# A two-layer encoder trunk on one core: the first layer's last columns as a pair, the V chunk first in the second mixer, and more of the couples' sums made ahead

## The chip, the cores and the metric

The kernel runs on one core of one Trainium2 chip, as one program. The metric is the device time of one execution in microseconds, the lower the better. TensorE is PE in the profile (PEld is its weight load), VectorE is DVE, ScalarE is ACT, GpSimd is POOL, and SyncE, which issues nearly all DMAs here, is SP.

## The reference, cut to what matters

The trunk has two layers on a sequence of 256 tokens with 2048 features, all float32. Layer 0 mixes tokens with a bidirectional mLSTM (8 heads), layer 1 with a bidirectional HGRN2 (16 heads). Behind each mixer stands a gated MLP of 5504 features with a convolution of width 3.

```python
def conv_glu(hn, w_up, conv_w, conv_b, w_down):
    u = hn @ w_up
    a, v = jnp.split(u, 2, axis=-1)
    ...
    c = conv_b
    for j in range(CONV_W):
        c = c + ap[:, j:j + s] * conv_w[j]
    return (jax.nn.gelu(c, approximate=False) * v) @ w_down

def reference(...):
    ...
    for layer in range(DEPTH):
        hn = rmsnorm(h, norm_mix_g[layer])
        if layer % N_MIXERS == 0:
            mix = mlstm_mixer(hn, ...)
        else:
            mix = hgrn_mixer(hn, ...)
        h = h + mix
        h = h + conv_glu(rmsnorm(h, norm_ffn_g[layer]), ffn_w_up[layer], ...)
    return rmsnorm(h, final_g)
```

The HGRN2 mixer projects its input to q, i (the values V), g (an output gate), and one forget gate for each direction. A forget gate f gives `k = (1 - lb) * sigmoid(-f)` and the decay `lb + (1 - lb) * sigmoid(f)`.

## The kernel before

**Products in two parts.** Every matrix product is made with operands that are split in two float32r parts, a high one and a low one, and three matmuls: high by high, high by low, low by high. Weights come from HBM as float32 (`raw`, 1 MB at a time, three buffers), ScalarE casts a piece of 128 x 1024 to the high part (`wh`, L144), and VectorE subtracts that from the piece (`wl`, L145). `LOOK = 3` such pieces are prepared ahead of TensorE.

**Chunks.** `stream` runs through a list of chunks, in the order in which TensorE executes them; each has a kind:

- "fm" (feature-major): 256 output features by 256 tokens, the weights stationary; for each k tile and each half of the features one matmul of 512 columns (L340) and one of 256 (L344). The entries of `swap` exchange two neighbours in this order.
- "tm" (token-major): 256 tokens by 512 output features, x stationary, 6 matmuls of 512 columns for each k tile (L356).
- "st" (a pair): 256 tokens by 1024 output features. Two k tiles by two blocks of 512 columns by two halves of the tokens form a unit. A plain unit takes 8 products of three matmuls; a unit listed in `seven` takes 7, by the scheme of Strassen and Winograd with 2 x 2 blocks (L231). For that it needs sums of the weight's blocks (the couples' sums, T1 to T4) and sums of the token blocks of x (`token_sums`, `SX`). Four PSUM banks (`psm`) hold the products P1, P6, P7, P5 that several outputs share, the four banks of the other pool (`psa`) the outputs' own sums. Behind the last unit of seven `mid` adds the shared products to the residual `hm` (L557 to L565); at the end `done` adds the rest (L570).

**The couples' sums** are either made in the pair itself, by `combine` (four subtractions on VectorE, L203), or ahead: `prepare` is a side job that loads a unit's four blocks (2 x 0.5 MB, `praw`), subtracts on VectorE (L603) and stores the result to a scratch tensor in HBM, `tscr`; the pair loads it again (`T<-tscr`). Before the change 22 units of layer 0 and 30 of layer 1 are made ahead, in lists: `early[layer]` runs beside the mixer of that layer (`prepare_early`), and each of the two parts of a layer's MLP has a list that runs beside its up chunks. The three units of each mixer's own pair (`SEVEN_MIX`) are made by `combine`.

**Side jobs.** Everything that isn't a chunk's main product is a Python generator on `Side`, and `side.tick` gives each its turn as the chunks are written, by a clock of planned microseconds (10.4 for an fm chunk). The periods of `prepare` and the steps of a head are in that time. The framework then schedules each engine's instructions; only those that are pinned keep their written order.

**The order of the work.** Layer 0: 16 chunks of the mixer; its output projection as a tm chunk, a pair for the middle 1024 columns (`mixed`), and a tm chunk; then the MLP in two parts of 22 and 21 tiles of 128 features (`FA`, `FB`): up chunks (fm), then the down projection over the part's tiles. In the first part this is a pair for columns 0 and 1 (of four of 512) and a pair for columns 2 and 3. In the second part it is a pair for columns 0 and 1 with six units of seven, and **two tm chunks** for columns 2 and 3 (`w_d2`). Layer 1 begins with its mixer (`hgrn`): four groups of four heads, each with six fm chunks, a V chunk after the third of them, and a G chunk after the sixth. Its output projection and its MLP follow as in layer 0, except that the last part ends in a second pair (`w_d3`) with seven units of seven.

**Norms.** When a column block of `hm` is final, `Norm.add` squares it on ScalarE (L509) and starts `turn`, which transposes it on TensorE (L417) into a bank of `psa` and splits it into the next x tiles, `xt` (ScalarE L362, VectorE L363). While a pair is running (`held`), `turn` waits, since the pair has all of `psa`.

**A head of the second mixer** takes its three projections (`take`), makes the gate `g` with a Sigmoid on ScalarE (L978) and a multiply-add on VectorE (L980), multiplies q by it on GpSimd (L981), then doubles its window seven times on VectorE (L1029), and ends in small matmuls.

Of the kernel before, what the change touches and what calls it, by code (L numbers as in the profile page):

```python
# [8 lines left out]
F32 = mybir.dt.float32  # L9
# [6 lines left out]
P = 128  # L16
T = 256
# [32 lines left out]
SEVEN = (1, 2, 3, 4, 6, 7, 8, 9), (1, 2, 4, 5, 7, 8)  # L50
SEVEN_END = (1, 2, 3, 4, 5, 6, 7)
# [4 lines left out]
QUAD = 32  # L56
LEVELS = (1, 2, 4, 8, 16, 32, 64)
# [5 lines left out]
def trunk_kernel(ctx, tc, xT, x_d, fg_d, pp_d, cst_d, w_gate, w_first, w_aq, w_ak, w_av, w_ao, w_aout, w_ao2,  # L63
                 w_bq, w_bv, w_bg, w_bout, w_bo2, w_up, w_d0, w_d1, w_d2, w_d3, out, mscr, tscr):
# [21 lines left out]
    def aux(name):  # L86
        return psa.tile([P, 512], F32, tag="aux", name=name)
# [40 lines left out]
    turns = dict(w=0)  # L128
# [92 lines left out]
    def squares_by_seven(ch, fetch, ready):  # L221
# [37 lines left out]
        for u in range(units):  # L259
# [27 lines left out]
            if u in ch.seven:  # L287
# [8 lines left out]
                if u == last:  # L296
                    ch.mid(psm_)
                continue
# [82 lines left out]
    class Norm:  # L381
# [166 lines left out]
    def pair(src, nk, c0, x, sums, norm, seven):  # L548
# [18 lines left out]
        def done(ps):  # L567
            for i in range(4):
                h = part(i // 2, i % 2)
                dve.tensor_tensor(h, h, ps[i], ALU.add)  # L570
            if norm is not None:
                norm.add(c0)
                side.push(second())
# [7 lines left out]
        ch.stored, ch.waits, ch.pool = {}, None, None  # L581
        return ch

    def prepare(tiles, todo, first, period, finished, start, ahead):
# [12 lines left out]
        for i, (_, dst) in enumerate(todo):  # L597
# [21 lines left out]
    def mixed(w, w2, x, norm, close):  # L619
# [8 lines left out]
        two = pair(w2, KT, 1, x, sums, norm, SEVEN_MIX)  # L628

# [299 lines left out]
    def hgrn(norm, nxt):  # L929
# [32 lines left out]
        def take(hd, what, ps):  # L962
# [17 lines left out]
            dve.tensor_scalar(g, g, oml[:, hd:hd + 1], lb[:, hd:hd + 1], ALU.mult, ALU.add)  # L980
# [110 lines left out]
        swaps = {(0, 1): (0, 6), (1, 0): (2, 24), (1, 2): (4,), (2, 0): (2, 24), (2, 2): (4,), (3, 0): (2,), (3, 2): (10,)}  # L1091
        heads = [dict() for _ in range(BH)]
        chunks = []
        for qd in range(BH // 4):
# [25 lines left out]
            chunks.append(Chunk("tm", w_bg[qd], KT, norm.x, done_g, paced=True))  # L1120
# [5 lines left out]
        return chunks + mixed(w_bout, w_bo2, yx, nxt, stack.close)  # L1126


    def ffn(layer, norm, nxt):
        stack = ExitStack()  # L1130
        ending = isinstance(nxt, FinalNorm)
        seven = SEVEN[0], SEVEN_END if ending else SEVEN[1]
        box = dict(n=(2 * len(SEVEN[0]) + len(SEVEN[1])) * layer)
        chunks, pairs = [], []
# [9 lines left out]
        def done_up(f, i, GT, SX, seven):  # L1144
            def go(ps):
# [18 lines left out]
                if i % 2 and i // 2 in seven:  # L1164
                    n = seven.index(i // 2)
                    if seven is not SEVEN[1]:
                        z = GT[i - 1][:, P:T], GT[i - 1][:, T + P:2 * T]
                    else:
                        if n % 3 == 0:
                            box["s4"] = mp.tile([P, 768], F32R, tag=f"sx{len(seven) + n // 3}", name="s4")  # L1170
                        z = tuple(box["s4"][:, (n % 3 * 2 + j) * P:(n % 3 * 2 + j + 1) * P] for j in range(2))
# [4 lines left out]
        for part, (f0, nf) in enumerate(((0, FA), (FA, FB))):  # L1176
            GT, SX, todo, finished = [], {}, [], []

# [7 lines left out]
            for i in range(nf):  # L1186
                chunks.append(Chunk("fm", w_up[layer, f0 + i], KT, norm.x, done_up(f0 + i, i, GT, SX, seven[part]),
# [150 lines left out]
```

## Time and profile before

| | us |
|---|---|
| median of 3 runs (lowest, highest) | 2385.79 (2384.44, 2386.21) |
| the profiled execution | 2384.87 |
| its span, first to last instruction | 2382.9 |
| TensorE busy in the span | 2365.6 |
| VectorE busy | 1938.4 |
| ScalarE busy | 1433.6 |
| GpSimd busy | 205.4 |

Stretches of the span, in us from its start: mixer 0 to 392 (its pair 326 to 367), up chunks of layer 0's first part 392 to 638, their pairs to 746, up chunks of the second part to 980, its pair to 1032, the two tm chunks to 1092, mixer 1 to 1608, its pair to 1656, up chunks of layer 1's first part 1680 to 1926, pairs to 2035, up chunks of the second part to 2268, pairs to the end.

In a row of the windows, the figures are: the stretch, its length, the busy time of PE, PEld, DVE, ACT and POOL with the number of instructions in brackets, the granted TensorE clock as a share, the share of time in which the DMA engines were busy, and GB/s. With one engine or one line asked for, its busy time alone stands there. In a row of the groups: line, engine, operation, output and inputs by the program's names, shapes, number; busy us, mean ns; idle us before them and who ended it. In a row of the timeline: start, us, engine, line, and in square brackets the idle time before. A wait's row has the total, the number and the longest.

### The profile page before, as it was taken

How to read it: one execution, taken by the hardware profiler on the slowest of the kernel's cores; microseconds unless marked ns; L12 is line 12 of the kernel's file. 1: busy time of each engine (PE TensorE's matmuls, PEld its weight loads, DVE VectorE, ACT ScalarE, POOL GpSimd, SP SyncE). 2: the span in 40 equal slices, each digit the busy share in tenths (PEclk: the TensorE clock that was granted, in tenths of full speed). 3: DMA queues.
4: the chain of work that ended last, by engine and by line, in shares of the span. 5: the costliest groups of instructions: out<-in, count | busy, mean ns of one | idle time of the engine just before them, and what ended most of it. 6: DMA issues, size and time to landing. Idle time of an engine off the chain costs nothing.

```text
span 2382.9 us, 38182 instructions
## 1 busy us (share of the span) xinstructions
PE 2365.6 (99%) x14572; PEld 2024.3 (85%) x14572; DVE 1938.4 (81%) x3001; ACT 1433.6 (60%) x2271; POOL 205.4 (9%) x242
## 2 busy tenths in 40 slices
PE   9999999999999999999999999999999999999998
PEld 7888888888888888888888888887888888888886
DVE  7777687888788887766888888888788788888787
ACT  7655456555665555655666666665555566455565
POOL 0100000000000000001233222320000000000000
PEclk9999999999999999999999999999999999999999
DMA  8777656886697885755666666764788588887695
GB/s 300 240 272 268 227 174 214 302 303 226 223 354 272 283 280 195 274 190 204 244 234 228 246 236 227 245 225 173 258 299 283 195 309 310 288 288 253 204 345 201
DMA packets 112471, 601.23 MB, mean 252 GB/s; under 512 B 12688, under 2 KB 13200, under 8 KB 66464
## 3 DMA queue, kind: packets, MB, share of 16 engines
q1 hardware_dynamic: 110592, 594.78, 71.1%
q0 software_dynamic: 1120, 3.21, 0.8%
q8 instruction: 114, 1.87, 0.3%
q10 hardware_dynamic: 576, 0.79, 0.1%
q14 instruction: 69, 0.57, 0.1%
HBM read 542.05 MB, written 56.69 MB: 251 GB/s over the span
## 4 chain that ended last, share of the span: by engine, by line
PE 95%; DVE 2%; DMA 1%; issue 1%; ACT 0%; SPq 0%; POOL 0%; DVEq 0%; POOLq 0%; ACTq 0%
PE mm L340 36%; PE mm L356 18%; PE mm L344 18%; PE pc L231 12%; PE mm L231 6%; DMA praw<-in_w_d 1%; PE py L1066 1%; PE pn L808 1%; DVE wl L145 1%; PE pd L1016 0%; PE pz L417 0%; PE pa L1016 0%; DVE QK L1029 0%; DMA Mb<-mscr 0%; DMA raw<-in_w_first 0%
## 5 line engine op out<-in xcount | busy, mean ns | idle before, releaser
L340 PE MATMUL mm<-xt,wh 128*128 128x512 f32 x3776 | 1314.2, 394 | 0.0
L145 DVE TENSOR_TENSOR wl<-raw,wh 128x1024 fp32r<-128x1024 f32 (+1 forms) x845 | 1034.6, 1229 | 274.6 <-ACT wh L144 268.9
L144 ACT CAST wh<-raw 128x1024 fp32r<-128x1024 f32 (+1 forms) x845 | 875.6, 1042 | 520.4 <-PE mm L340 293.6
L344 PE MATMUL mm<-xt,wl 128*128 128x256 f32 x3776 | 1046.3, 278 | 0.0
L340 PEld LDWEIGHTS mm<-xt,wh 128*128 128x128 f32 x3776 | 706.2, 188 | 160.1
L344 PEld LDWEIGHTS mm<-xt,wl 128*128 128x128 f32 x3776 | 709.7, 188 | 4.5 <-issue 0.4
L356 PE MATMUL mm<-wh,xt 128*128 128x512 f32 x1024 | 320.5, 391 | 2.2 <-ACT xt L362 1.6
L231 PE MATMUL pc<-wh,g 128*128 128x512 f32 x676 | 228.0, 389 | 0.0
L356 PEld LDWEIGHTS mm<-wh,xt 128*128 128x128 f32 x1024 | 191.1, 188 | 41.8 <-ACT xt L362 2.0
L356 PE MATMUL mm<-wl,xt 128*128 128x512 f32 x512 | 197.9, 391 | 0.0
L603 DVE TENSOR_TENSOR praw<-praw 128x512 f32<-128x512 f32 x208 | 143.8, 691 | 49.4 <-DMA praw<-in_w_d 39.0
L231 PEld LDWEIGHTS pc<-wh,g 128*128 128x128 f32 x676 | 126.9, 188 | 26.4
L231 PE MATMUL pc<-wl,g 128*128 128x512 f32 x338 | 131.5, 389 | 0.0
L145 DVE TENSOR_TENSOR wl<-T,wh 128x1024 fp32r<-128x1024 f32 (+1 forms) x116 | 110.2, 961 | 20.2 <-ACT wh L144 19.5
L231 PE MATMUL mm<-wh,sx 128*128 128x512 f32 x348 | 124.4, 391 | 0.0
L144 ACT CAST wh<-T 128x1024 fp32r<-128x1024 f32 (+1 forms) x116 | 96.2, 836 | 45.8 <-PE pc L231 20.3
L564 POOL TENSOR_TENSOR hm<-hm,u 128x512 f32<-128x512 f32 x9 | 12.6, 1395 | 1186.4 <-DVE u L563 592.3
L1029 DVE TENSOR_TENSOR QK<-QK,G 128x256 f32<-128x256 f32 x224 | 109.7, 537 | 5.4 <-ACT kq L1008 5.0
L356 PEld LDWEIGHTS mm<-wl,xt 128*128 128x128 f32 x512 | 96.2, 188 | 19.1
L1150 ACT COPY avc<-mm 128x256 f32<-128x256 f32 x172 | 64.2, 373 | 78.2 <-PE mm L344 78.2
L1008 ACT COPY kq<-QK 128x512 f32<-128x512 f32 x112 | 74.5, 669 | 57.3 <-DVE QK L1029 44.6
L1151 DVE TENSOR_TENSOR avc<-mm,avc 128x256 f32<-128x256 f32 x172 | 71.9, 418 | 12.7 <-ACT avc L1150 12.6
(247 smaller groups left out, 2322.3 us busy)
## 6 DMA issues: line engine op xcount, KB each, us to landing
raw<-in_w_up SPq DMA_DIRECT2D x172, 1024.0 KB, 5.4
praw<-in_w_d SPq DMA_DIRECT2D x104, 512.0 KB, 6.8
tscr<-praw SPq DMA_DIRECT2D x104, 512.0 KB, 6.8
raw<-in_w_bq SPq DMA_DIRECT2D x48, 1024.0 KB, 5.0
raw<-in_w_d SPq DMA_DIRECT2D x52, 768.0 KB, 6.1
T<-tscr SPq DMA_DIRECT2D x52, 768.0 KB, 7.7
raw<-in_w_d SPq DMA_DIRECT2D x32, 1024.0 KB, 5.2
raw<-in_w_ao SPq DMA_DIRECT2D x24, 1024.0 KB, 4.9
```

What stands on the lines that cost most here:

```text
L144: pin(act.copy(wh[:, :m], r))
L145: pin(dve.tensor_tensor(wl[:, :m], r, wh[:, :m].bitcast(F32), ALU.subtract))
L231: pe.matmul(ps, a, b, start=id(ps) not in begun, stop=stop and i == 2)
L340: pe.matmul(ps[f], wh[:, c:c + P], x, start=k + kk == 0, stop=False)
L344: pe.matmul(ps[f][:, 0:T], wl[:, c:c + P], x[:, 0:T], start=False, stop=k + kk == ch.nk - 1)
L356: pe.matmul(ps[t], x[:, a + t * P:a + (t + 1) * P], w[:, c], start=st and i == 0, stop=sp and i == 2)
L603: dve.tensor_tensor(out, x, y, ALU.subtract)
L808: pe.matmul(pn[:, 0:258], w, v, start=(i == 0), stop=(i == len(parts) - 1))
L1008: act.copy(m, blocks(QK, h))
L1029: dve.tensor_tensor(two[:, j], two[:, j], by[:, j], ALU.mult)
L1150: act.copy(z, p[:, T:2 * T])
L1151: dve.tensor_tensor(z, p[:, 0:T], z, ALU.add)
```

## The change

1. Layer 0's last two tm chunks become a pair (`w_d3` for both layers; `w_d2` goes), with seven units of seven; the pair before it has seven instead of six. `SEVEN` is now the same for both layers.
2. `SPLIT` says in which lists the last pair's units are made ahead: in layer 0 none beside the mixer, 2 beside the first part's up chunks, 5 beside the second's; in layer 1 2, 2 and 3 (before: 7 beside the mixer). The three units of mixer 1's pair are now made ahead too, in `early[1]`. In numbers, layer 0's lists go from 8, 8, 6 to 8, 10, 12, layer 1's from 15, 8, 7 to 13, 10, 10.
3. `prepare` spreads a list over all of its time: the last third of a period, which only `prepare_early` waited for, is waited for everywhere.
4. Since layer 0's last pair gives two column blocks at once, `turn` may use the four banks of `psm` once the last unit of seven is behind it (`ch.rest`), and `done` calls `norm.add` for the first block as soon as that one is added.
5. In the second mixer the V chunk of the first group comes first, and V and G chunks stand ahead of the fm chunks with the numbers in `TMS`; `swap` is set by the same list. From the third V chunk on the order of the chunks is the one before.
6. The gate's multiply-add moves from VectorE to ScalarE.
7. In the mixers' pairs the temporaries of `combine` and of `token` get buffers of their own.

```diff
-SEVEN = (1, 2, 3, 4, 6, 7, 8, 9), (1, 2, 4, 5, 7, 8)
-SEVEN_END = (1, 2, 3, 4, 5, 6, 7)
+SEVEN = (1, 2, 3, 4, 6, 7, 8, 9), (1, 2, 3, 4, 5, 6, 7)
+SPLIT = (0, 2, 5), (2, 2, 3)
...
+TMS = (0, 4, 8, 11, 15, 18, 21)
...
     def temporary(pool_, name):
-        return pool_.tile([P, 1536], F32, tag="avc", bufs=TEMP if pool_.name == "ff" else 2, name=name)
+        ff = pool_.name == "ff"
+        return pool_.tile([P, 1536], F32, tag="avc" if ff else name, bufs=TEMP if ff else 2, name=name)
...
-        side.until(lambda: ch.waits is None or ch.waits)
+        side.until(lambda: all(ch.waits))
...
                 if u == last:
                     ch.mid(psm_)
+                    ch.rest = ch.ends
...
         def turn(self, c):
             yield 2.5
-            while held:
+            while held and not held[-1].rest:
                 yield 1.0
             for k0 in (4 * c, 4 * c + 2):
-                pz = aux("pz")
+                pz = psm.tile([P, 512], F32, tag="mm", name="pz") if held else aux("pz")
...
         def done(ps):
-            for i in range(4):
-                h = part(i // 2, i % 2)
-                dve.tensor_tensor(h, h, ps[i], ALU.add)
+            for c in range(2):
+                for t in range(2):
+                    h = part(t, c)
+                    dve.tensor_tensor(h, h, ps[2 * t + c], ALU.add)
+                if norm is not None and c == 0:
+                    norm.add(c0)
             if norm is not None:
-                norm.add(c0)
                 side.push(second())
...
             for j in range(2):
                 nc.sync.dma_start(dst[:, j * 1024:(j + 1) * 1024], loaded[i][j])
+            yield period / 3
             if not ahead:
-                yield period / 3
                 load(i + 1)
...
+    def store(ch, src, u, todo):
+        ch.stored[u] = tscr[turns["t"]]
+        turns["t"] += 1
+        todo.append((src[:, 2048 * u:2048 * (u + 1)], ch.stored[u]))
+
-    def mixed(w, w2, x, norm, close):
+    def mixed(w, w2, x, norm, close, layer=None):
...
         two = pair(w2, KT, 1, x, sums, norm, SEVEN_MIX)
+        if layer is not None:
+            for u in SEVEN_MIX:
+                store(two, w2, u, early[layer][0])
+            two.waits = [early[layer][1]]
...
-            dve.tensor_scalar(g, g, oml[:, hd:hd + 1], lb[:, hd:hd + 1], ALU.mult, ALU.add)
+            act.activation(g, g, AF.Identity, bias=lb[:, hd:hd + 1], scale=oml[:, hd:hd + 1])
...
-        swaps = {(0, 1): (0, 6), (1, 0): (2, 24), (1, 2): (4,), (2, 0): (2, 24), (2, 2): (4,), (3, 0): (2,), (3, 2): (10,)}
...
+            vs.append(Chunk("tm", w_bv[qd], KT, norm.x, done_v, begin if qd == 0 else None, paced=True))
+            gs.append(Chunk("tm", w_bg[qd], KT, norm.x, done_g, paced=True))
             for i in range(6):
-                if i == 3:
-                    chunks.append(Chunk("tm", w_bv[qd], KT, norm.x, done_v, paced=True))
...
-                chunks.append(Chunk("fm", w_bq[6 * qd + i], KT, norm.x, done_i, begin if not chunks else None,
-                                    swap=swaps.get((qd, i), (1, 13) if i == 3 else ()), paced=True))
+                n = 6 * qd + i
+                fs.append(Chunk("fm", w_bq[n], KT, norm.x, done_i, swap=(2, 13) if n in TMS else (4, 15), paced=True))
...
-            chunks.append(Chunk("tm", w_bg[qd], KT, norm.x, done_g, paced=True))
+        for n, ch in enumerate(fs):
+            if n in TMS:
+                i = TMS.index(n)
+                chunks.append((vs, gs)[i % 2][i // 2])
+            chunks.append(ch)
+        chunks.append(gs[3])
...
-            def two(src, c0, norm, seven, todo=todo, finished=finished, GT=GT, SX=SX, nf=nf):
+            def two(src, c0, norm, seven, shares, GT=GT, SX=SX, nf=nf):
                 ch = pair(src, nf, c0, lambda k: GT[k], lambda u: SX[u], norm, seven)
...
+                ch.waits, left = [], list(seven)
+                for n, (todo, finished) in zip(shares, [early[layer]] + lists):
+                    for u in left[:n]:
+                        store(ch, src, u, todo)
+                    if n:
+                        ch.waits.append(finished)
+                    left = left[n:]
...
-                chunks += project(lambda c: w_d2[c % 2], nf, lambda k, GT=GT: GT[k], nxt)[2:]
+            chunks.append(two(w0, 0, nxt if part else None, SEVEN[part], (0, 0, n) if part else (n, 0)))
+            chunks.append(two(w1, 2, nxt if part and not ending else None, SEVEN[part], SPLIT[layer] if part else (0, n)))
+            if part:
+                chunks[-1].last = ending
+                if ending:
+                    chunks[-2].before, chunks[-1].half = nxt.load, nxt.half
+                else:
+                    chunks[-1].ends = True
```

More of the change, by code (lines that the diff above doesn't have):

```diff
@@ L580, in pair @@
         ch.mid, ch.seven, ch.sums = mid, seven, sums
-        ch.stored, ch.waits, ch.pool = {}, None, None
+        ch.stored, ch.waits, ch.pool, ch.ends, ch.rest = {}, (), None, False, False
         return ch
@@ L1131, in ffn @@
         ending = isinstance(nxt, FinalNorm)
-        seven = SEVEN[0], SEVEN_END if ending else SEVEN[1]
-        box = dict(n=(2 * len(SEVEN[0]) + len(SEVEN[1])) * layer)
-        chunks, pairs = [], []
+        box = {}
+        chunks, pairs, lists = [], [], []
         def begin():
@@ L1165, in go @@
                     n = seven.index(i // 2)
[L1166 to L1171, printed above, removed]
+                    z = GT[i - 1][:, P:T], GT[i - 1][:, T + P:2 * T]
                     SX[i // 2] = token_sums(mp, n, box["c"], c, avc[:, 0:2 * T], z)
@@ L1197, in two @@
+                assert not left
                 pairs.append(ch)
                 return ch
-            chunks.append(two(w_d0[layer][:, f0 * 1024:(f0 + nf) * 1024], 0, nxt if part else None, seven[part],
-                              *(() if part else early[layer])))
-            if not part:
-                chunks.append(two(w_d1[layer], 2, None, seven[0]))
-            elif ending:
-                chunks[-1].before = nxt.load
-                chunks.append(two(w_d3, 2, None, seven[1], *early[layer]))
-                chunks[-1].last, chunks[-1].half = True, nxt.half
-            else:
-                chunks += project(lambda c: w_d2[c % 2], nf, lambda k, GT=GT: GT[k], nxt)[2:]
+            w0, w1 = w_d0[layer][:, f0 * 1024:(f0 + nf) * 1024], w_d3[layer] if part else w_d1[layer]
@@ L1308, in layout @@
         w_d0=np.stack([squares(d[:, :, 0:2]) for d in down]), w_d1=np.stack([squares(d[:FA, :, 2:4]) for d in down]),
-        w_d2=np.ascontiguousarray(down[0, FA:, :, 2:].transpose(2, 1, 0, 3)).reshape(2, P, FB * 512),
-        w_d3=squares(down[1, FA:, :, 2:]),
+        w_d3=np.stack([squares(d[FA:, :, 2:]) for d in down]),
     )
```

21 lines of the change are left out of this document (9 added, 12 removed).

## The prediction

> **What bounds the kernel now.** I read the page first: the share of each engine, then the chain that ended last.
>
> ```profile
> span 2382.9 us, 38182 instructions
> PE 2365.6 (99%) x14572; PEld 2024.3 (85%) x14572; DVE 1938.4 (81%) x3001; ACT 1433.6 (60%) x2271; POOL 205.4 (9%) x242
> ...
> PE 95%; DVE 2%; DMA 1%; issue 1%; ACT 0%; SPq 0%; POOL 0%; DVEq 0%; POOLq 0%; ACTq 0%
> ```
>
> TensorE is 95% of the chain, so a matmul that goes is time that goes, and another engine counts only where it makes TensorE wait. The profile is of an execution of 2384.87 us: its span and 1.97 us around it. The median of the three runs, 2385.79 us, is 0.92 us above that; I work the change out against the profiled execution and add the 0.92 at the end.
>
> What does one matmul of 512 columns cost? Not its mean duration of 389 ns, since they overlap. Next come the windows, of a stretch in which nothing but a pair's products run, and the groups of the chunks that the change replaces.
>
> ```profile
> 985.00:1030.00 45.00, 45.00 (x200) 1.00 0.78 278
> ```
>
> ```profile
> L356 PE MATMUL mm<-wh,g 128*128 128x512 f32 x168 | 53.2, 394 | 0.0
> ...
> L356 PE MATMUL mm<-wl,g 128*128 128x512 f32 x84 | 32.7, 389 | 0.0
> ```
>
> A window counts what overlaps it, so the 200 began within 45 us and one duration of 0.389 us: 45.39 / 200 = 0.227 us each. The two lower rows are the two token-major chunks that end layer 0 today: 168 + 84 = 252 matmuls.
>
> Where does TensorE wait? I went through the span by stage. Two stages that do the same work differ, the mixers' pair in the first and in the second layer (first two rows); the third row is the bad part of the second, and behind it stand who waited in that stage and the longest gap.
>
> ```profile
> 326.00:367.00 41.00, 41.00 (x183) 33.95 (x182) 39.18 (x57) 24.49 (x30) 0.00 (x0) 1.00 0.56 195
> 1608.00:1656.00 48.00, 46.09 (x194) 36.53 (x193) 43.18 (x65) 24.48 (x31) 0.00 (x0) 0.96 0.49 170
> ...
> 1632.00:1640.00 8.00, 6.23 (x19) 4.23 (x19) 8.00 (x12) 5.88 (x7) 0.00 (x0) 0.79 0.25 70
> ```
>
> ```profile
> ACT wh L144 <- DVE raw L203: 3.7, 2, 2.7
> PEld pc L231 <- ACT wh L144: 3.2, 3, 2.0
> ```
>
> ```profile
> 1634.67 0.50 PE L231 MATMUL pc<-wh,yb 128*128 128x512 f32 x1 [1.56 <-ACT wh L144]
> ```
>
> VectorE (the third busy figure) is full for 8.00 of 8.00 us from 1632. The couples' sums (L203) hold it; ScalarE's casts of the weights wait for a sum that is written into `raw`, and TensorE's weight loads wait for the casts. The gap of 1.56 us cost the clock too: 0.79 granted in those 8 us, 1.00 in the sister stage.
>
> **The change part by part.**
>
> *Matmuls.* A unit in `seven` has 7 products of 3 matmuls instead of 8. The new last pair of layer 0 covers 21 k tiles with 7 such units: 7 x 21 + 3 x 24 + 12 = 231 matmuls for 252. The pair before it goes from 6 such units to 7: 3 fewer. 24 x 0.227 = 5.4 us, all on the chain. The transposes stay as many, and layer 1's counts stay.
>
> *The second mixer's pair.* Twelve instructions of L203, as large as those of L603 in the next fence, 12 x 0.691 = 8.3 us, leave the 48 us in which VectorE is busy for 43.18; the sums come loaded instead. All that is lost there today: 194 matmuls began within 48.39 us and should take 194 x 0.227 = 44.0, so 4.4 us. Idle time is 1.9 of it (48 - 46.09) and the clock 1.7 (0.21 of 8 us). Nothing that I see comes in its place: the sister stage has VectorE at 39.18 of 41 us with such sums still inside, and TensorE idles 0. The bounds of the gain are 0 (the loaded sums come late, rival B) and 4.4; I take 4.0, near the sister's row.
>
> The Trainium skill (TensorE: Matmul & The Clock Gate, Part 1: The HAM clock gate) puts the halving of the clock behind an idle window of about 3.4 us. Here the trace differs: a gap of 1.56 us with some shorter ones was enough. By the rule this stage would lose 1.7 us less and the sum below would be smaller by as much; the measured clock decides.
>
> *Sums made ahead.* Each stored unit is four instructions of L603 with two loads before and two stores behind, all issued on SP.
>
> ```profile
> L603 DVE TENSOR_TENSOR praw<-praw 128x512 f32<-128x512 f32 x208 | 143.8, 691 | 49.4 <-DMA praw<-in_w_d 39.0 <-issue 9.8
> ...
> L540 DVE TENSOR_TENSOR avc<-avc 128x128 f32<-128x128 f32 x116 | 33.6, 290 | 2.9
> ...
> L542 DVE TENSOR_TENSOR sx<-avc,sx 128x384 fp32r<-128x384 f32 x29 | 16.0, 550 | 0.0
> ```
>
> ```profile
> 746.00:980.00 234.00, 234.00 (x1351) 204.57 (x1350) 190.98 (x291) 129.38 (x200) 3.57 (x2) 1.00 0.74 251
> 412.00:560.00 148.00, 148.00 (x856) 129.44 (x855) 127.29 (x207) 83.91 (x132) 0.00 (x0) 1.00 0.84 296
> 1093.00:1560.00 467.00, 466.09 (x4206) 402.71 (x4206) 396.82 (x680) 316.50 (x595) 137.69 (x165) 1.00 0.67 235
> 1926.00:2035.00 109.00, 109.00 (x483) 90.17 (x482) 92.86 (x100) 71.98 (x83) 3.55 (x2) 1.00 0.88 319
> ```
>
> ```profile
> 412.00:560.00 148.00, 20.53 (x30) 1.00 0.84 296
> ```
>
> 208 / 4 = 52 units become 63: 8 more in layer 0 and the mixer's 3. The up chunks of layer 0's second part (746 to 980) go from 6 to 12 units: 24 x 0.691 = 16.6 us, and one more token sum, 4 x 0.290 + 0.550 and a split of 128 columns at about 0.29, 2.0 us. VectorE there: 190.98 + 18.6 = 209.6 of 234 us, 0.90. The other three up parts take 2 or 3 units more, but spread them over all of their chunks and no longer over two thirds of them (the third of a period in `prepare` now counts for them too), so they get no denser. Is 0.90 too much? The densest such stretch of today is 412 to 560 (the last row counts L603's instructions alone): 0.86 with 30 of them in 148 us, 0.203 a us, and TensorE idles 0. Twelve units over 192 of the planner's microseconds, about 206 real ones (234 for 21 chunks planned at 10.4), are 0.233 a us: 0.86 + 0.030 x 0.691 = 0.88. DMA: a unit moves 128 x 2048 x 4 bytes each way, 2.1 MB; 0.0076 units a us more are 16 GB/s, 312 after 296, below the 319 of the pairs of layer 1's first part, where TensorE idles 0 too. On SP a store waits for VectorE, and the loads of weights behind it wait along; three `raw` buffers stand in between. The bounds are 0 and 3.3 us (one gap as at 1634 with its slow clock); I take 0.3, near the row of 412. If that cover is gone, it is rival C.
>
> *The boundary of the layers.* The last pair gives columns 2 and 3 together, so 8 and no longer 4 of the second mixer's x tiles are made after the last matmul. Its first chunk is now V, which needs tile 8 after 8 x 6 x 0.227 = 10.9 us and tile 15 after 20.4. How long it takes is seen behind the pair that stands before the last one today, in the order of time:
>
> ```profile
> 1022.59 0.59 ACT L557 COPY u<-mm 128x512 f32<-128x512 f32 x1 [1.45 <-PE mm L231]
> ...
> 1029.61 0.68 DVE L563 TENSOR_TENSOR u<-u,mm 128x512 f32<-128x512 f32 x1
> ...
> 1032.68 2.46 DVE L570 TENSOR_TENSOR hm<-hm,pc 128x512 f32<-128x512 f32 x4
> ...
> 1038.93 0.48 DVE L363 SCALAR_TENSOR_TENSOR xt<-pz,pp,xt 128x256 fp32r<-128x256 f32 x1 [0.33 <-ACT xt L362]
> ...
> 1050.49 0.48 DVE L363 SCALAR_TENSOR_TENSOR xt<-pz,pp,xt 128x256 fp32r<-128x256 f32 x1
> ```
>
> The pair's sums are added from 1032.68, so its last matmul began at 1032.3. The first tile is there 7.1 us after that, the eighth 18.7: inside the deadlines by 3.8 and 1.7 us, though nothing pressed for them. Tiles 0 to 7 are made during the last 13.6 us of the new pair (60 matmuls) in the four banks that `mid` frees, the last of them 7.7 us after `mid` begins (1022.59 to 1030.29). TensorE works in order, so a transpose put ahead of its bank or its sum holds every product behind it. Bounds 0 to 4 us; I take 0.6, since the row leaves slack everywhere.
>
> *The second mixer's order and its gate.*
>
> ```profile
> L1155 ACT ACTIVATE avc<-avc,pp 128x256 f32<-128x256 f32 x86 | 51.5, 599 | 45.5 <-DVE avc L1153 45.2
> ...
> L980 DVE TENSOR_SCALAR G<-G,oml,lb 128x256 f32<-128x256 f32 x32 | 15.7, 492 | 0.5 <-ACT G L978 0.5
> ...
> L1158 ACT ACT_TABLE_LOAD x2 | 2.6, 1283 | 0.0
> ```
>
> From the third V chunk on the order is the old one. In the row of 1093, VectorE loses L980's 15.7 us and two early units (8 x 0.691 = 5.5): 375.6 of 467 us, 0.80. ScalarE gets 32 x 0.599 = 19.2, each in front of the casts queued behind it: 335.7, 0.72. Neither binds. TensorE idles 467 - 466.09 = 0.9 us there in all, so no more can be won; a new order can lose some. Bounds -0.9 and +3; I take 0. An Identity might want another table than Sigmoid, 64 loads of 1.283 us; but L1155's 86 Identities beside as many Gelus (L1158) needed 2 loads. The Trainium skill (ScalarE: Activation LUTs, Table sets: the hidden batching unit) has identity in every set; beside Gelu the trace agrees, beside Sigmoid no run here shows it.
>
> **Sum.** -5.4 - 4.0 + 0.3 + 0.6 + 0 = -8.5 us: 2376.4 for the profiled execution, 2377.3 for the median.
>
> **The rivals.** A: TensorE waits at the layers' boundary for tile 8 or for a bank. For it: eight tiles in a queue behind the pair's sums; against it: 3.8 us of slack. A gap and its slow clock, 1.6 + 1.7, and a short one: 4 us, 2381. B: the second mixer's pair stays late, because its loaded sums go into memory that the heads have only just left. Against it: the pair wants the first of them only after two units, 10.9 us, and DMA is at 0.49 there. The 4.0 are not won: 2381. C, slower: VectorE becomes the bound in the up chunks of layer 0's second part. It decides where VectorE falls behind by more than the three pieces of weights made ahead (a piece is 8 matmuls of 512 and 8 of 256 columns, 12 x 0.227 = 2.7 us, so 8 us). For it: 0.88 to 0.90 is above every stretch of up chunks today. Each of the 7 token sums would bring a gap of 1.6 us and 1.7 of slow clock, 7 x 3.3 = 23 us: 2400. The table loads would be a smaller form of it, 82 us more on ScalarE's 336 of 467.
>
> **How the numbers follow.** Forecast 0.69, A 0.11, B 0.10, C with the tables 0.10. The forecast's own span goes from 2375 (5.4 + 4.4 + 0.9 won and nothing lost) to 2380 (3 us lost again, in the up chunks or in the second mixer). I add 2.5 below, for pauses too short to show as idle time, which a new order can win as well; above, A and B with such a loss reach 2384. C is left out. A measurement of this kernel tells about 0.2%, 4.8 us, from no change: faster means under 2381.0. The forecast does, and A and B in 0.06 each: 0.81; 0.09 lie within, 0.10 are slower.
>
> **What would show it.** Right: 14548 matmuls, 252 of L603's instructions, a clock of 1.00 and no waits of weight loads for `wh` in the second mixer's pair, VectorE near 0.90 and TensorE without idle time in layer 0's second up chunks. Wrong: a gap over 1 us, with a clock under 1.00 behind it, in those up chunks or within 25 us of layer 0's last pair, or more table loads in the second mixer than its two.

## The result and the profile after

The changed kernel takes 2379.96 us, the median of 10 runs, against 2384.70 us for the kernel before (10 runs, 2383.15 to 2388.31): a ratio of 0.9976, 95% interval 0.9966 to 0.9986, and the medians are 4.7 us apart. The forecast was 8.5 us less. One run of the changed kernel, at 3236.56 us with a granted clock of 0.677, is left out of the ratio (the median of the other nine is 2379.77 us). The profiled execution took 2380.58 us, its span 2378.3 (before 2384.87 and 2382.9).

The page of the changed kernel, its head, the chain that ended last and the group of the sums (L608, before L603):

```profile
span 2378.3 us, 38347 instructions
PE 2360.9 (99%) x14548; PEld 2019.2 (85%) x14548; DVE 1965.4 (83%) x3028; ACT 1459.1 (61%) x2321; POOL 203.9 (9%) x244
...
PE 94%; DMA 3%; DVE 2%; issue 1%; ACT 0%; SPq 0%; POOL 0%; DVEq 0%; POOLq 0%; ACTq 0%
...
L608 DVE TENSOR_TENSOR praw<-praw 128x512 f32<-128x512 f32 x252 | 174.5, 692 | 26.4 <-DMA praw<-in_w_d 21.7
```

14548 matmuls and 252 sums are the announced counts. TensorE's share of the chain fell and DMA's rose from 1% to 3%: loads of stored sums (`T` from `tscr`) now stand in it. The windows of the changed kernel by stage: layer 0's second up chunks, its two end pairs, the V chunk behind them, the second mixer, its pair, and the first 25 us of the pairs of layer 0's and layer 1's first part.

```profile
746.00:980.00 234.00, 234.00 (x1351) 204.50 (x1350) 204.31 (x321) 130.66 (x202) 3.55 (x2) 1.00 0.87 302
980.00:1087.00 107.00, 107.00 (x481) 88.67 (x481) 92.64 (x103) 72.66 (x92) 7.97 (x4) 1.00 0.85 309
1087.00:1111.00 24.00, 24.00 (x117) 19.89 (x116) 16.72 (x36) 15.70 (x28) 0.69 (x1) 1.00 0.48 157
1087.00:1606.00 519.00, 516.24 (x4682) 443.42 (x4681) 423.46 (x718) 365.43 (x698) 144.33 (x177) 1.00 0.64 222
1606.00:1650.00 44.00, 43.65 (x193) 35.53 (x193) 36.11 (x53) 24.56 (x33) 0.00 (x0) 1.00 0.69 241
625.00:650.00 25.00, 24.65 (x127) 20.66 (x126) 19.04 (x32) 14.80 (x26) 0.00 (x0) 1.00 0.89 299
1908.00:1932.00 24.00, 23.38 (x120) 19.65 (x119) 18.01 (x31) 13.65 (x24) 0.00 (x0) 1.00 0.86 299
```

And the kernel before in the second mixer and at the start of the same two pairs:

```profile
1093.00:1608.00 515.00, 514.09 (x4674) 442.96 (x4674) 436.21 (x752) 349.25 (x659) 148.48 (x177) 1.00 0.67 234
625.00:650.00 25.00, 25.00 (x130) 21.26 (x129) 18.16 (x31) 14.11 (x24) 0.00 (x0) 1.00 0.74 259
1908.00:1933.00 25.00, 25.00 (x137) 21.55 (x136) 20.53 (x33) 15.08 (x25) 0.00 (x0) 1.00 0.77 267
```

TensorE is busy throughout the first three stages of after. It idles 2.8 us in the second mixer (before 0.9) and 0.35 and 0.62 us where layer 0's and layer 1's first pairs begin (before 0.00). From the first to the last matmul of each stage, in us (transposes at a mixer's end are left out):

| stage | before | after | difference | forecast |
|---|---|---|---|---|
| start and first mixer | | | -0.2 | 0 |
| layer 0, first part's pairs | 108.6 | 109.3 | +0.6 | 0 |
| layer 0, second part's up chunks | 232.8 | 232.8 | 0 | +0.3 |
| layer 0's end, to the next mixer's first matmul | 113.0 | 106.6 | -6.4 | -5.4 |
| second mixer, V chunk and boundary included | 515.4 | 519.5 | +4.1 | +0.6 |
| second mixer's pair | 47.6 | 43.6 | -3.9 | -4.0 |
| layer 1, first part's pairs | 108.7 | 109.9 | +1.2 | 0 |

Differences are taken before rounding; together they are the span's 4.6 us. The expectations below count the second mixer's pair from 0.2 us earlier, as 47.8 and 43.9. The -6.4 holds 0.9 us of transposes (6.38 - 24 x 0.227) which did not go: those of four x tiles now run inside the V chunk and count in the mixer, whose own loss is therefore 4.1 - 0.9 = 3.2 us.

So both gains came in their size, and 5.0 us went again at two places: the second mixer (3.2) and the first parts' pairs (1.8, of which 1.5 within their first 48 matmuls). The waits of TensorE in the second mixer, after and then before (engine, line and releaser; us in total, times, longest):

```profile
PE pd L1030 <- issue: 1.1, 1, 1.1
PE pz L1101 <- DVE y L1095: 0.8, 1, 0.8
PE mm L343 <- issue: 0.7, 1, 0.7
```

```profile
PE pd L1016 <- issue: 0.7, 1, 0.7
PE py L1066 <- ACT V L1100: 0.2, 1, 0.2
```

The middle wait of after is new. Its place in the timeline of after, in the second G chunk:

```profile
1383.80 0.16 DVE L516 TENSOR_SCALAR rs<-ss 128x2 f32<-128x2 f32 x1
1384.04 1.60 POOL L517 TENSOR_TENSOR rs<-rs,mhalf 128x2 f32<-128x2 f32 x1 [0.71 <-DVE rs L516]
1385.94 0.97 DVE L1095 SCALAR_TENSOR_TENSOR y<-y,rs,sg 128x128 f32<-128x128 f32 x2
...
1386.63 0.66 PE L1101 MATMUL pz<-cst,y 128*128 128x128 f32 x2 [0.84 <-DVE y L1095]
```

TensorE's transpose of a finished head's `y` (L1101) stands in its order ahead of the products, but the head's scale is still on its way: VectorE to GpSimd (1.60 us there) and back to VectorE.

### The profile page after: what moved, and what is told of

The parts are those of the page before. It is cut to its first block, busy times and chain, and to the rows that moved or that the text cites. A ratio compares the mean times of both kernels' runs of the same rounds, so it can differ in the third digit from the quotient of the medians.

```text
span 2378.3 us, 38347 instructions
## 1 busy us (share of the span) xinstructions
PE 2360.9 (99%) x14548; PEld 2019.2 (85%) x14548; DVE 1965.4 (83%) x3028; ACT 1459.1 (61%) x2321; POOL 203.9 (9%) x244
## 4 chain that ended last, share of the span: by engine, by line
PE 94%; DMA 3%; DVE 2%; issue 1%; ACT 0%; SPq 0%; POOL 0%; DVEq 0%; POOLq 0%; ACTq 0%
PE mm L343 36%; PE mm L347 18%; PE mm L359 16%; PE pc L233 13%; PE mm L233 7%; DMA T<-tscr 1%; DMA praw<-in_w_d 1%; DVE wl L146 1%; PE pn L822 1%; PE py L1080 1%; PE pd L1030 0%; PE pz L420 0%; PE pa L1030 0%; DMA Mb<-mscr 0%; ACT wh L145 0%
## 5 line engine op out<-in xcount | busy, mean ns | idle before, releaser
L233 PE MATMUL pc<-wh,g 128*128 128x512 f32 x776 | 262.8, 390 | 0.0
L608 DVE TENSOR_TENSOR praw<-praw 128x512 f32<-128x512 f32 x252 | 174.5, 692 | 26.4 <-DMA praw<-in_w_d 21.7
L233 PEld LDWEIGHTS pc<-wh,g 128*128 128x128 f32 x776 | 145.6, 188 | 30.2
L233 PE MATMUL pc<-wl,g 128*128 128x512 f32 x388 | 150.9, 389 | 0.0
L233 PE MATMUL mm<-wh,sx 128*128 128x512 f32 x396 | 141.6, 390 | 1.0 <-ACT wh L145 1.0
L146 DVE TENSOR_TENSOR wl<-T,wh 128x1024 fp32r<-128x1024 f32 (+1 forms) x132 | 125.8, 965 | 16.4 <-ACT wh L145 16.2
L145 ACT CAST wh<-T 128x1024 fp32r<-128x1024 f32 (+1 forms) x132 | 109.4, 835 | 46.4 <-PE pc L233 19.9
L233 PEld LDWEIGHTS mm<-wh,sx 128*128 128x128 f32 x396 | 74.2, 188 | 17.1 <-ACT wh L145 1.8
```

Of the source, the lines that this page charges most:

```text
L145: pin(act.copy(wh[:, :m], r))
L146: pin(dve.tensor_tensor(wl[:, :m], r, wh[:, :m].bitcast(F32), ALU.subtract))
L233: pe.matmul(ps, a, b, start=id(ps) not in begun, stop=stop and i == 2)
L608: dve.tensor_tensor(out, x, y, ALU.subtract)
```

## The experiments

Five questions, twelve kernels. Edits are to the changed kernel unless it says before; every ratio is to the kernel before, run on the same chip.

**Where does the second mixer lose 3 us: the order of the chunks, the exchanges, or the gate?**

`e1_order`: the V chunk stays first, the other chunks go back to their old places.

```diff
-TMS = (0, 4, 8, 11, 15, 18, 21)
+TMS = (0, 6, 9, 12, 15, 18, 21)
```

> The changed kernel with V first, but the other V and G chunks of the second mixer back where they stood before (TMS = 0, 6, 9, 12, 15, 18, 21). Theory 'order': the new places of G and V chunks cost the 3.2 us by which the second mixer grew (515.4 us to 519.5, less 0.9 for transposes that moved into it), so the mixer comes back to about 516.5 and the time falls by 3 us. Rival 'gate': the mixer stays at 519. Rival 'chance of the instruction fetch' (pauses of TensorE with nothing to wait for, 2.2 us after against 0.9 before): they move to other places, and the mixer lands anywhere from 517 to 520.

Measured: 2375.95 us (0.9968, 0.9956 to 0.9981), 4.0 less than the changed kernel. The intervals of the two ratios overlap, but all five runs (2375.20 to 2377.41) lie below the nine of the changed kernel (2377.53 to 2380.58). The mixer takes 516.5 us, 3.0 less, without the wait at L1101. It is the order or the exchanges, which `swap` ties to it; `e9_swap` parts them.

`e2_gate`: the gate's multiply-add on VectorE again.

```diff
-            act.activation(g, g, AF.Identity, bias=lb[:, hd:hd + 1], scale=oml[:, hd:hd + 1])
+            dve.tensor_scalar(g, g, oml[:, hd:hd + 1], lb[:, hd:hd + 1], ALU.mult, ALU.add)
```

> The changed kernel with the gate's multiply-add back on VectorE. Theory 'order': no gain, the second mixer stays at 519 or grows by up to 1 us, because VectorE has 15.7 us more. Rival 'gate' (0.6 us more in front of ScalarE's casts cost the 3.2): the mixer falls to 516.5 and the time by 3 us.

Measured: 2379.86 us (0.9981, 0.9972 to 0.9990), the same as the changed kernel; the mixer takes 518.9 us, and the wait at L1101 is there (0.4 us). The gate's engine is neutral.

`e9_swap`: `e1_order`, with the exchanges (`swap`) of the changed kernel. Since `swap` is set by `TMS`, e1 had changed both.

```diff
-TMS = (0, 4, 8, 11, 15, 18, 21)
+TMS = (0, 6, 9, 12, 15, 18, 21)
-swap=(2, 13) if n in TMS else (4, 15), paced=True))
+swap=(2, 13) if n in (0, 4, 8, 11, 15, 18, 21) else (4, 15), paced=True))
```

> V first and the other V and G chunks in their old places, as in the run of the old places, but with the exchanges of neighbouring matmuls at the fm chunks where the change has them. Theory 'order': the places alone made the difference, the second mixer stays near 516.5 us (517.5 at most) and the time near 2376. Rival 'exchanges': they had moved with the places and were what won, the mixer goes back to 519 and the time to 2379.

Measured: 2376.36 us (0.9966, 0.9954 to 0.9978); the mixer takes 516.3 us. The exchanges do nothing; the places do.

`e10_g1`: of the places, only that of the second G chunk goes back (exchanges as in the change).

```diff
-TMS = (0, 4, 8, 11, 15, 18, 21)
+TMS = (0, 4, 8, 12, 15, 18, 21)
```

> The changed kernel with the second G chunk alone moved back by one fm chunk (ahead of the thirteenth instead of the twelfth), exchanges as in the change. In the changed kernel the waits of TensorE stand behind that chunk's new place: at 1385 us transposes wait for a head's y, at 1407 and 1458 the instruction fetch. Theory 'second G': the mixer falls by 2 us or more, to 517.5. Rival 'the long blocks of four fm chunks' (the first eight fm chunks): it stays at 519.

Measured: 2376.33 us (0.9964, 0.9952 to 0.9977); the mixer takes 515.7 us. The same window of the changed kernel, of e1 and of e10:

```profile
1086.00:1603.00 517.00, 514.24 (x4674) 441.77 (x4673) 422.63 (x715) 363.45 (x693) 143.63 (x176) 1.00 0.64 223
```

```profile
1086.00:1603.00 517.00, 516.38 (x4688) 444.49 (x4687) 426.61 (x720) 365.31 (x699) 146.09 (x177) 1.00 0.65 224
```

```profile
1086.00:1603.00 517.00, 516.98 (x4691) 444.71 (x4690) 427.35 (x720) 365.63 (x699) 141.83 (x177) 1.00 0.65 224
```

TensorE's idle time goes from 2.76 to 0.62 and 0.02 us. One number in `TMS` decides it. The wait at L1101 is in every trace with the second G chunk ahead of the 12th fm chunk (after and e2, e3, e4, e6: 0.4 to 1.7 us) and in none with the old place. It is about 1 us of the 3; most of the rest is pauses that no semaphore ended (last section). Over all traces with V first the mixer takes 518.9 to 520.7 us with the second G chunk's new place and 515.7 to 518.3 with the old one.

**How does the layers' boundary stay free, and what would it cost?**

`e8_fmfirst`: the second mixer begins with an fm chunk, which wants all x tiles for its first products, and the first V chunk goes to its old place.

```diff
-TMS = (0, 4, 8, 11, 15, 18, 21)
+TMS = (3, 6, 9, 12, 15, 18, 21)
-norm.x, done_v, begin if qd == 0 else None, paced=True))
+norm.x, done_v, paced=True))
-done_i, swap=(2, 13) if n in TMS else (4, 15), paced=True))
+done_i, begin if n == 0 else None,
+                                swap=(2, 13) if n in TMS else (4, 15), paced=True))
```

> The changed kernel with the second mixer beginning with an fm chunk as before, V ahead of the fourth. An fm chunk wants x tile 8 after 5.6 us and tile 15 after 10.5; behind the old pair the first new tile took 7.1 us and the eighth 18.7. Theory 'V first covers the boundary': TensorE waits 2 to 8 us in the first fm chunk, with a half clock behind it, and the time rises by 1 to 7 us over that of the old places (2376). Rival: the tiles come faster when they are wanted, the wait is under 1 us, and the time is 2376.

Measured: 2379.13 us (0.9977, 0.9968 to 0.9986). The boundary cost about 1.0 us, in which TensorE waited for parts of the weights (`wh`, `wl`) and not for a tile, and the mixer takes 517.3, 0.8 more than in e1: the V chunk first is worth about 1 us. The wait is at the rival's bound, the time within the theory's. What the other 2.4 us between the medians are is not shown; the profiled execution lost 1.9 in its first 18 us, which the edit does not touch.

`e12_norest`: `e1_order`, and `turn` waits for the pair's end as before (the four banks of `psm` are not used).

```diff
-                    ch.rest = ch.ends
+                    ch.rest = False
```

> V and G in their old places, but the transposes of columns 0 and 1 may not use the banks that mid frees (ch.rest stays false): all 16 x tiles of the second mixer are made behind the pair. This takes away the cover that the prediction counted on. The first tile behind a pair took 7.1 us before, so theory 'cover' expects TensorE to wait about 5 to 7 us at the start of V, a half clock of 1.7 us more, and a time of 2381 to 2385. Rival 'the tiles come faster when they are wanted' (as with fm first, where the wait was 1 us): 2 to 4 us, 2378 to 2380.

Measured: 2376.76 us (0.9968, 0.9955 to 0.9980). Pair and V chunk take 131.7 us, 1.2 more than e1's 130.5. Neither number was met: eight more tiles made after the last matmul delay the next chunk by only 1.2 us. The 7.1 us of the expectation are of tiles that needed the sums of the pair just ended. The first eight tiles here come from columns that were final before this pair, so their transposes begin right behind its last matmul (1084.48), at 1084.71, and V at 1085.88. What it would cost to make all tiles from a pair's own sums is not shown by this run.

**What holds the second mixer's pair: the couples' sums or the shared temporaries?**

`e4_mixer`: the sums of the second mixer's pair are made inside it again.

```diff
-stack.close, 1)
+stack.close)
```

> The changed kernel with the sums of the second mixer's pair made in the pair again, nothing loaded. If these sums were what stopped TensorE there, the stretch from the pair's first to its last matmul goes from 43.9 us back to about 47.8 with a half clock inside, and the time rises by 4 us. Rival: the order of work around the pair (the new temporaries' buffers, fewer sums beside the heads) had freed it, and the stretch stays at 44 to 45.

Measured: 2381.39 us (0.9986, 0.9977 to 0.9995), 1.4 more than the changed kernel and not 4. The pair takes 44.7 us, 1.1 more than in after and 2.8 less than before, and no half clock: the rival holds.

`e5_temps`: the kernel before, with own buffers for the temporaries of `combine` and `token` and nothing else.

```diff
-        return pool_.tile([P, 1536], F32, tag="avc", bufs=TEMP if pool_.name == "ff" else 2, name=name)
+        ff = pool_.name == "ff"
+        return pool_.tile([P, 1536], F32, tag="avc" if ff else name, bufs=TEMP if ff else 2, name=name)
```

> The kernel before with one edit: in the mixers' pairs the temporaries of the couples' sums and of the token sums get buffers of their own. With the sums made in the pair again the changed kernel took 44.8 us there and not 47.8, so theory 'shared buffers' (two buffers for six users let two units' sums run as one block of 8 instructions) expects 44 to 45.5 us in the second mixer's pair, no half clock, and a time 3 us below before. Rival 'fewer sums beside the heads' (13 or 10 and not 15 units) expects the pair to stay near 47.8 and the time the same.

Measured: 2381.56 us (0.9989, 0.9980 to 0.9997), 2.7 less than before. The pair takes 44.8 us: 2.8 of the 3.9 us come from this one line. VectorE's timeline shows how: before, eight of the twelve subtractions L203 stand together from 1631.6 to 1637.6 us, with one split of a weight piece among them; in e5 no two stand together, and the splits that TensorE wants run in between.

`e6_shared`: the changed kernel with the old, shared temporaries (the same edit backwards).

> The changed kernel with the old shared temporaries in the mixers' pairs, the three units' sums still loaded. Theory 'shared buffers': only three sums are left that take turns with the token sums and no subtraction among them, so the pair stays at 43.9 to 45 us and the time within 1 us of the changed kernel; either half of the edit is then enough. If the pair goes back over 46 us, the buffers alone were the cause and the loads add nothing.

Measured: 2386.23 us (1.0008, 0.9999 to 1.0017), 6.3 more than the changed kernel and not within 1. The pair takes 46.0 us: the loads alone give 1.6 of the 3.9 us. ScalarE's cast there waits 3.8 us for a loaded sum (`T` from `tscr`), a wait that after's pair does not have. Windows of the pair, before, then e4, e5 and e6, each ahead of its TensorE waits there (L231, L232 and L233 are one line):

```profile
1607.00:1652.00 45.00, 43.09 (x180) 34.08 (x179) 39.79 (x62) 25.26 (x32) 0.11 (x1) 0.96 0.48 170
...
PE pc L231 <- ACT wh L144: 1.8, 2, 1.6
```

```profile
1607.00:1652.00 45.00, 43.57 (x192) 35.37 (x192) 41.55 (x65) 24.90 (x32) 0.00 (x0) 1.00 0.52 183
...
PE pc L233 <- DVE wl L146: 1.4, 1, 1.4
```

```profile
1607.00:1652.00 45.00, 44.00 (x192) 35.46 (x191) 42.06 (x64) 24.54 (x31) 0.00 (x0) 1.00 0.51 177
...
PE pc L232 <- ACT wh L144: 1.0, 2, 0.5
```

```profile
1607.00:1652.00 45.00, 42.92 (x187) 34.34 (x186) 36.08 (x54) 25.21 (x32) 0.00 (x0) 1.00 0.63 228
...
PE mm L232 <- ACT wh L145: 1.3, 1, 1.3
PE pc L232 <- DVE wl L146: 0.5, 1, 0.5
```

With the sums inside and own buffers (e4, e5), VectorE is fuller than before, 41.6 and 42.1 of 45 us, and yet TensorE idles only 1.4 and 1.0 us and the clock stays at 1.00. With the sums loaded and shared buffers (e6) VectorE has 9 us to spare and TensorE idles 2.1. Only both edits together come down to after's 0.35. e6's profiled execution is 4.7 us longer than after's. The pair adds 2.4, and 4.4 are in layer 1's first up chunks; other stages are shorter by some 2. In those up chunks the next matmul begins on average 236.0 ns behind one of 512 columns instead of 231.7, and 117.3 ns behind one of 256 instead of 115.0. That stage, after and then e6, has no idle time and the full clock in e6, only fewer matmuls:

```profile
1690.00:1935.00 245.00, 244.38 (x1391) 212.74 (x1390) 208.06 (x333) 138.72 (x218) 0.00 (x0) 1.00 0.82 280
```

```profile
1690.00:1935.00 245.00, 245.00 (x1377) 212.00 (x1376) 205.72 (x330) 135.14 (x215) 0.00 (x0) 1.00 0.82 278
```

Why is open: the temporaries there are the same in both kernels, and this is one trace.

**What holds the first parts' pairs?** In after, waits from 640 to 650 us, then SyncE's wait ahead of these loads (L196) from 610 to 650 us, and the links of the chain of waits where the two pairs begin (start, us):

```profile
ACT wh L145 <- DMA T<-tscr: 1.9, 1, 1.9
...
PEld mm L233 <- ACT wh L145: 0.8, 1, 0.8
```

```profile
SPq L196 <- DVE avc L1168: 4.2, 2, 4.0
```

```profile
640.04 0.34 DVE avc L1168
640.38 0.60 DVE wl L146
641.00 6.57 DMA T<-tscr
...
1923.43 7.16 DMA T<-tscr
```

The cast waits for a stored sum. Its load lands 6.6 and 7.2 us after its issue, and it is issued 3.5 and 3.2 us behind the pair's first matmul (637.5 and 1920.3), since the loaded sum takes a buffer (`avc`) that VectorE's work on the last up chunk (L1168) still holds. The sum itself had long been stored: the first of the two pairs takes sums that are made beside the mixer.

`e3_sooner`: in `prepare`, the first parts' lists are spread over 30 planner's microseconds less.

```diff
-todo, 18.0, (nf * 10.4 - 26.0) / len(todo), finished, late, True))
+todo, 18.0, (nf * 10.4 - (56.0 if nf == FA else 26.0)) / len(todo), finished, late, True))
```

> The changed kernel with the couples' sums beside the first part's up chunks of both layers finished 30 planned us earlier (56 instead of 26 left at the end). Theory 'late finish': the gaps of 0.5 and 0.8 us at the start of the first part's pairs (stages 0.6 and 1.2 us longer than before) come from the last stores and the pair's first loads meeting on the DMA engines (busy 0.89 and 0.86 there, 0.74 and 0.78 before); both gaps go, 1.8 us less. Rival 'buffers': the second load waits for the temporaries of the last up chunk whatever the DMAs do, the gaps stay, no change in time.

Measured: 2377.74 us (0.9975, 0.9966 to 0.9984). The two stages take 108.6 and 108.8 us again, and the windows have no idle time:

```profile
625.00:650.00 25.00, 25.00 (x128) 21.20 (x127) 18.87 (x30) 15.92 (x26) 0.00 (x0) 1.00 0.74 263
1908.00:1932.00 24.00, 24.00 (x121) 20.34 (x121) 17.14 (x26) 14.18 (x24) 0.00 (x0) 1.00 0.70 239
```

DMA falls from 0.89 and 0.86 to 0.74 and 0.70, as before the change. The load in question is issued 1.5 us behind the pair's first matmul at all four places of e3 and e7 (`e7_best` below has the same edit), as before the change in layer 0. In the other traces with the change's lists it is 2.0 to 4.3 us, at 19 places. In the 12 of them where it is 3.0 or less the first 48 matmuls lose under 0.1 us; in the 7 where it is 3.1 or more they lose 0.1 to 1.1. So the late load fits every loss there. The share of the DMA engines does not: e1 has 0.89 in the same window of layer 0 and no idle time. Theory and rival are each half right: it is the buffer that the load waits for, and the earlier end of the sums brings the load forward. What makes the up chunk's temporaries late is not shown.

The edit's worth in time is not shown either. Three traces without it (e1, e6 and e10) lose nothing at either start. Over the whole stage, layer 0's pairs take 0 (e1) to some 1.5 us (e2) more than before in kernels that do not differ ahead of them, and part of that is lost where the second of the two pairs begins, which this run does not settle. The 2.2 us to the changed kernel are within the intervals.

**What is a matmul of the pairs worth, and what do the repairs give together?**

`e11_plain`: `e1_order`, and layer 0's last pair has one unit of seven and no longer seven: 18 matmuls more, 14566. The six plain units read x tiles whose place the token sums have taken, so this kernel multiplies other numbers there.

```diff
-            chunks.append(two(w1, 2, nxt if part and not ending else None, SEVEN[part], SPLIT[layer] if part else (0, n)))
+            one = part and not ending
+            chunks.append(two(w1, 2, nxt if one else None, (7,) if one else SEVEN[part],
+                              (0, 0, 1) if one else SPLIT[layer] if part else (0, n)))
```

> V and G in their old places, and the first layer's last pair with one unit of seven instead of seven (the last one, which the freed banks need): 18 more matmuls of 512 columns, six units' sums less. If TensorE's count is the time there, the two pairs at the end of layer 0 take 106.4 + 18 x 0.227 = 110.5 us and the whole 2376 + 4.1 = 2380. Rival: the loads and sums of these units cost part of it elsewhere, and without them the time rises by less than 3 us.

Measured: 2381.94 us (0.9988, 0.9980 to 0.9997). The two end pairs take 110.4 us against 106.4 in e1: 4.0 / 18 = 0.22 us a matmul, as forecast (0.227). The median rose by 6.0, though. In the profiled executions, which are 4.5 apart, the second mixer takes 1.8 more (518.3 us instead of 516.5), where the order is e1's and only the pauses at the end of this document grew, and the time up to layer 0's first pair 1.3 less.

`e7_best`: the edits of `e1_order` and `e3_sooner`.

> The changed kernel with both edits that won: V and G back in their old places behind the first V (second mixer 516.5 us, 3 less) and the first part's sums finished 30 planned us earlier (pairs at 108.6 to 108.8 us each). If the gains add up the time is 2374 to 2376 us. If the gaps at the pairs' start come and go by chance, it is that of the first edit alone, 2376, with a spread of 1 us.

Measured: 2375.51 us (0.9963, 0.9950 to 0.9975), 8.8 less than before, the fastest of all; that it beats e1 (0.4 us) is within the scatter, so it does not tell whether the second edit adds anything. The mixer takes 515.8 us.

## Why the prediction was right or wrong

*Matmuls (-5.4): right.* Counts as announced, no idle time in the end pairs, and e11 measured 0.22 us each.

*The second mixer's pair (-4.0): size right (-3.9), mechanism mostly wrong.* I read VectorE full and put the gap down to the couples' sums. e5 kept all twelve sums, had VectorE as full, and won 2.8 us: what made the difference was the two buffers on which `combine` and `token` took turns. That edit stood in the diff (point 7) and I gave it no term. Loading the sums gives 1.6 alone (e6: 47.6 - 46.0) and 1.1 beside own buffers (e4: 44.7 - 43.6). That the term came out at its size is in good part luck: without point 7, for which it had no term, it would have been 1.6. Rival B did not occur; after's pair has no wait for the loads.

*The clock.* Before, a gap of 1.56 us halved it for 3.4 us, so the stage's 1.7 us of clock were real, and in after they are won. Between its start and TensorE's last matmuls, a half clock stands in only two traces more, each time for 3.4 us: behind a gap of 1.71 us at L1101 in e4, and of 1.91 us near 10 us in e8. The Trainium skill (TensorE: Matmul & The Clock Gate, Part 1: The HAM clock gate) has an idle window of about 3.4 us; the measured gaps decide against it once more. The length of the gap alone does not decide, though: every gap up to 1.48 us kept 1.00 (1.43 in e4's pair), but so did one of 1.59 us, longer than the 1.56, at 8.45 us before the change.

*Up chunks of layer 0's second part (+0.3): right, rival C absent.* VectorE 204.31 of 234 us is 0.87 (0.90 forecast), DMA 302 (312), TensorE idles 0. But I looked for the cost of the added sums only there. "They get no denser" speaks of the other three up parts' middle and misses their end, where the pair's loads wait for the last up chunk's buffers. Both first parts' pairs became longer, by 1.8 us together in this trace, and that had no term in the sum.

*Boundary (+0.6): nearly nothing, rival A absent.* The V chunk has no idle time. Its cover is thinner in price than I made it: without it 1.0 (e8) or 1.2 us (e12) are lost. Rival A's 4 us are not met in either run.

*The second mixer's order and gate (0, with a bound of +3): the step that failed.* It cost 3.2. I checked that no engine binds (VectorE 0.82, ScalarE 0.70 in the window) and took 0. What decided was a single place: "from the third V chunk on the order is the old one" is true, but the second G chunk comes in front of that, one chunk earlier (e10). There a head's `y` was still on its way, which is about 1 us; the rest is pauses of TensorE that no wait explains. Shares of engines say nothing on either; for the first, the chain VectorE, GpSimd, VectorE, TensorE would have had to be followed to the time at which it is wanted. The forecast's range held this loss, but 4.7 us are little more than half of 8.5.

*Table loads: none added.* The second mixer has two before and two after, at 1.3 us; the Trainium skill's sentence that identity is in every set (ScalarE: Activation LUTs, Table sets: the hidden batching unit) holds beside Sigmoid as well.

## What to carry to other kernels

When a chunk moves in a TensorE queue written out by hand, follow the latest input of every small instruction that is inserted into it; a wait on a round trip over GpSimd shows up in no engine's share. Before blaming a full engine for a wait, ask which buffer the waiting instruction needs and who else takes turns on it: one tag was worth 2.8 us. The same question is worth asking of a load: data that was stored long ago still comes late when the buffer that it goes into is held by the stage before. Here such a load took 6.6 to 7.2 us to land, and every start of a first part's pair at which it was issued more than 3 us behind the first matmul lost time.

## What the runs showed of the hardware

TensorE pauses for 0.2 to 1.4 us with nothing to wait for ("issue") in the second mixer. In after:

```profile
1408.42 0.26 PE L1030 MATMUL pd<-kq 128*32 128x32 f32 x6 [1.11 <-issue]
```

```profile
1458.92 0.62 PE L343 MATMUL mm<-xt,wh 128*128 128x512 f32 x2 [0.74 <-issue]
```

The 14 traces have 18 such pauses of over 0.15 us in this stage, none to three in each. In all of them a packet of 16 KB of the queue that brings instructions had begun 1.1 to 2.6 us ahead of the pause (1406.0 and 1455.9 here), and TensorE went on 2.2 to 3.0 us after the packet's beginning; by chance a pause would lie so close behind one in less than one case of five (36 packets in 519 us of after). Each pause lies in a head's burst of 132 matmuls of 32 to 128 columns, with as many weight loads, or up to 7 us behind it. The queue, of which most packets cause no pause:

```profile
q8 instruction: 114, 1.87, 0.3%
```

That TensorE runs out of fetched instructions there fits all of this, and the expectations of e1 and e10 call it the instruction fetch; no run tested it by itself. The pauses come and go with the chunks' places: the one at 1406 to 1408 us, of 1.05 to 1.35 us, is in four of the five traces with the second G chunk's new place (after, e2, e3 and e6) and in none with the old one. Between e1 and e11 they also moved with 18 matmuls added to the pair ahead of the mixer. So some 2 us of a change to this stage can be the luck of where they fall. They may also be most of what the second G chunk's place cost beyond the 1 us at L1101.
